# A transformer layer on one core: the first feature block's shift by one-column TensorE products, c spread from a 4 KB row, another order at the start

## The chip, the cores and the metric

The kernel runs on one core of a Trainium2 chip. Its time is the device time of one execution in microseconds (us). Beside it stands the profile of one execution: a hardware record of what each engine did and when. The engines are TensorE (PE; its weight loads are listed as PEld), VectorE (DVE), ScalarE (ACT), GpSimd (POOL) and SyncE (SP), which here only issues DMAs. Each engine works through its own instructions in the order in which they stand in the program, and waits on semaphores for others.

## The reference

One layer of a diffusion transformer over 1024 tokens of 1024 features, with 256 context tokens. Only its beginning matters here:

```python
mod = jax.nn.silu(c) @ w_mod[l] + b_mod[l]
shift1, scale1, gate1, shift2, scale2, gate2 = jnp.split(mod[:, None, :], N_MOD, axis=-1)
...
h = x * (1.0 + scale1) + shift1
...
proj = h @ w_in + b_in
q_b = _rope_2d(_qk_rms(heads(OFF_QB, OFF_KB, B_HEADS), q_norm_g), rope)
```

`c` is one vector of 1024 numbers. A shift and a scale are needed for each of the 1024 features before a feature of `h` exists, and `h` is the operand of every projection. The projection that comes first in the kernel is that to the queries of the global branch (512 columns).

## The kernel before, in words

`x` lies transposed: features on the 128 partitions in KT = 8 blocks of 128 features, tokens along the free axis. Each block `k` of this first stage goes through the same steps.

- **Loads (`load1`, `load_w`, all from SP).** `wm0_k` and `wm1_k` are the columns of `w_mod` that make the shift and the scale of block `k`, 128 x 1024 numbers or 512 KB each; `xr_k` is the block of x, 512 KB; `wr_k` is the block of the projection's weights, 256 KB. So a block needs 1.75 MB. The loads of blocks 0 to 2 are issued at once and those of block `k + 3` while block `k` is worked on. A load waits for one of eight semaphore lanes (that is, for the load eight places ahead of it to have landed), and for its buffer.
- **Products (`product(j, k)`, on DVE, line 193).** Shift (j = 0) and scale (j = 1) of block `k` are sums over 1024 products per partition: `wm` times `sc`, where `sc` holds silu(c) on every partition alike. The result is one column of `modc`, with the bias from `bmc`. Each is one long instruction and a short one that reads its accumulator.
- **Spreading c.** `spread_load` loads the 4 KB row of `c` onto all 128 partitions, half from SP's queue and half from ACT's, 512 KB in all (line 182), and ACT takes the silu (line 185).
- **The affine step (`modulate(k)`).** ACT writes `hh_k` = x * scale + shift rounded to the matmul type (line 241, `high`), and the same unrounded back into `xr_k` (line 242). DVE subtracts the two into `hl_k`, the remainder (line 245, `low`). The weights are split in the same way into a high part (`whqb`) and a low part (`wlqb`). For block 0 the split is on DVE and POOL, for the others on ACT and DVE.
- **Matmuls.** For each block there are 24 of 128 x 512: for eight groups of 128 tokens the products hh x wh, hh x wl and hl x wh, which add up in eight PSUM tiles `q1acc0` to `q1acc7` over the eight blocks: 192 in the stage. They go by halves: four token groups (hh x wh, hh x wl by turns, lines 303 and 304, then four hl x wh, line 306), then the other four.
- **Ahead of them**, PE runs 28 matmuls of ones into `q1acc7` (line 280), whose result is overwritten.

The order on every engine here is the order of the code, written out by hand (a region with a manual schedule), so a diff of code is a diff of the engines' queues. After the stage come the gate products (`g`, lines 90 to 92), whose weights are split on ACT (`whg`) and POOL (`wlg`).

Of the kernel before, what the change touches and what calls it, by code (L numbers as in the profile page):

```python
# [7 lines left out]
F32 = mybir.dt.float32  # L8
R32 = mybir.dt.float32r
AF = mybir.ActivationFunctionType  # L10
ALU = mybir.AluOpType
# [58 lines left out]
def layer_kernel(  # L70
    ctx: ExitStack,
    tc: tile.TileContext,
    xT, ctxT, c_row, cc_row, wmodT, bmod, w_kv, w_qa, w_qb, w_g, b_kv, b_qa, b_qb, b_g,
    sink, qg, kg, w_a, w_b, w_out, ln1, ln2, ln2_row, w_up, conv, convb, w_dn,
    rope_c, rope_s, ident_in, mask_in, out,
):
# [127 lines left out]
    wr1 = {}  # L204

    def load1(k):
        wm = []
        for j in (0, 1):
            w = tmp(f"wm{j}_{k}")
            nc.sync.dma_start(w, wmodT[j * 8 + k])  # L210
            wm.append(w)
        x = tmp(f"xr{k}")
        if k == 0:
            nc.sync.dma_start(x[:, 0:HALF], xT[k][:, 0:HALF])
            load_w(0)
            nc.sync.dma_start(x[:, HALF:T], xT[k][:, HALF:T])
        else:
            nc.sync.dma_start(x, xT[k])
        if k + 1 < KT:
            load_w(k + 1)  # L220
        st1[k] = wm, x

    def product(j, k):
# [2 lines left out]

    def modulate(k):
        last = k + 1 == KT
        if k:
            if not last:  # L230
                w0.append([ph1.tile([P, 512], R32, tag="wp", name=f"w{a}qb{k + 1}", bufs=8) for a in "hl"])
                nc.scalar.copy(w0[-1][0], wr1[k + 1])
            if k > 1:
                product(1, k)
# [5 lines left out]
        def high(s):  # L240
            nc.scalar.activation(hh[:, s], x[:, s], AF.Identity, bias=a, scale=b)
            nc.scalar.activation(x[:, s], x[:, s], AF.Identity, bias=a, scale=b)

        def low(s):
            nc.vector.tensor_tensor(out=hl[:, s], in0=x[:, s], in1=hh[:, s].bitcast(F32), op=ALU.subtract)

        if k == 0:
            product(1, 0)
            w = [ph1.tile([P, 512], R32, tag="wp", name=f"w{a}qb0", bufs=8) for a in "hl"]
            split(wr1[0], *w, nc.vector, nc.gpsimd)  # L250
            w0.append(w)
            high(slice(0, HALF))
            high(slice(HALF, T))
            product(0, 1)
            low(slice(0, HALF))
            product(1, 1)
            low(slice(HALF, T))
            w0.append(wsplit(wr1[1], "qb1"))
        else:
            high(slice(0, T))  # L260
            if not last:
                nc.vector.tensor_tensor(out=w0[-1][1], in0=wr1[k + 1], in1=w0[-1][0].bitcast(F32), op=ALU.subtract)
# [6 lines left out]
    loads.enter_context(tc.manual_schedule(engines={E.SP, E.PE, E.DVE, E.Activation, E.Pool}))  # L269
    nc.scalar.dma_start(bmc, bmod)  # L270
# [4 lines left out]
    nc.vector.tensor_scalar(out=bmc[:, 8:16], in0=bmc[:, 8:16], scalar1=1.0, scalar2=None, op0=ALU.add)  # L275
    for k in (1, 2):
        load1(k)
    acc = [acc_tile(f"q1acc{t}") for t in range(NT)]
    for _ in range(NWARM):
        nc.tensor.matmul(acc[-1][:, 0:P], onesf, onesf, start=True, stop=True)  # L280
    w0 = []
    product(0, 0)
    modulate(0)
    mtmp = pw("mtmp")
    for k in range(KT):
        if k + 3 < KT:
            load1(k + 3)
        if k == 5:
            spread_load(cc_row, 1, (nc.sync,))
            bias_qb = bias_tile(b_qb, "bias_qb")  # L290
        if k + 1 < KT:
            modulate(k + 1)
        else:
            spread(scc, 1)
        h, w = hT[k], w0[k]
        for a in (0, 4):
            ts = [slice(t * P, (t + 1) * P) for t in range(a, a + 4)]
            if k == KT - 1:
                for t, s in enumerate(ts):
                    mm3(acc[a + t], (h[0][:, s], h[1][:, s]), w, False, True)  # L300
                continue
            for t, s in enumerate(ts):
                nc.tensor.matmul(acc[a + t], h[0][:, s], w[0], start=k == 0, stop=False)
                nc.tensor.matmul(acc[a + t], h[0][:, s], w[1], start=False, stop=False)
            for t, s in enumerate(ts):
                nc.tensor.matmul(acc[a + t], h[1][:, s], w[0], start=False, stop=False)

    def constants():
        nc.sync.dma_start(bgc, b_g)
# [1520 lines left out]
def _arrange(i):  # L1830
    import numpy as np

    def A(a):
        return np.ascontiguousarray(a)

    x = np.asarray(i["x"])[0]
    ctx = np.asarray(i["ctx"])[0]
    w_mod = np.asarray(i["w_mod"])[0]
    w_in = np.asarray(i["w_in"])[0]
    b_in = np.asarray(i["b_in"])[0]  # L1840
    w_up = np.asarray(i["w_up"])[0]
# [32 lines left out]
    a = dict(  # L1874
        xT=A(x.T).reshape(KT, P, T),
        ctxT=A(ctx.T).reshape(KT, P, NC),
        c_row=A(np.asarray(i["c"])[0]),
        cc_row=A(np.asarray(i["c_ctx"])),
        wmodT=A(w_mod.T).reshape(48, P, D),
        bmod=A(col(np.asarray(i["b_mod"])[0])),  # L1880
        w_kv=A(w_in[:, kv]).reshape(KT, P, 512),
        w_qa=A(w_in[:, qa]).reshape(KT, P, 512),
        w_qb=A(w_in[:, qb]).reshape(KT, P, 512),
        w_g=A(tiles(w_in[:, 1536:])),
        b_kv=A(b_in[kv]),
        b_qa=A(b_in[qa]),
        b_qb=A(b_in[qb]),
        b_g=A(col(b_in[1536:])),
        sink=A(np.asarray(i["attn_sink"])[0]),
        qg=A(np.asarray(i["q_norm_g"])[0]),  # L1890
        kg=A(np.asarray(i["k_norm_g"])[0]),
        w_a=A(pair(np.asarray(i["w_branch_a"])[0])),
        w_b=A(pair(np.asarray(i["w_branch_b"])[0])),
        w_out=A(tiles(np.asarray(i["w_out"])[0])),
        ln1=A(np.concatenate([col(np.asarray(i["ln1_g"])[0]), col(np.asarray(i["ln1_b"])[0])], 1)),
        ln2=A(np.concatenate([col(np.asarray(i["ln2_g"])[0]), col(np.asarray(i["ln2_b"])[0])], 1)),
        ln2_row=A(np.stack([np.asarray(i["ln2_g"])[0], np.asarray(i["ln2_b"])[0]])).reshape(2, 2, HALF),
        w_up=A(up),
        conv=A(cw.reshape(3, 2 * NF, P).transpose(2, 1, 0)),
        convb=A(col(np.asarray(i["conv_b"])[0])),  # L1900
        w_dn=A(dn),
        rope_c=A(cs.reshape(NT, P, HD).transpose(1, 0, 2)),
        rope_s=A(sn.reshape(NT, P, HD).transpose(1, 0, 2)),
        ident_in=np.eye(P, dtype=np.float32),
        mask_in=A(mask),
    )
    return a
# [29 lines left out]
```

## Time and profile before

| what | value |
|---|---|
| three runs | 1523.26, 1525.3, 1524.3 us; median 1524.3 |
| the profiled execution | 1523.1 us, of which the span of the instructions is 1521.3 us |
| granted TensorE clock in it | 0.997 |
| DVE, ACT, POOL busy | 77%, 52%, 49% of the span |
| HBM read and written | 179.45 MB, 65.86 MB |

The span runs from the first to the last instruction; the profiled execution's own time holds 1.8 us around it. A row of the timeline gives the start, the busy time, the engine, the line and operation, the written tile and the read ones with their shapes, how many rows are merged, and in brackets how long the engine sat idle ahead of it and what released it. `f32 x1` at the end is the type and the count.

### The profile page before, as it was taken

Reading aid. Unit: us, or ns where it says so; the run is one execution under the profiler, and the core shown is the slowest. Engines: PE = TensorE matmul, PEld = TensorE weight load, DVE = VectorE, ACT = ScalarE, POOL = GpSimd, SP = SyncE. Lnnn points to the kernel's source line nnn. Section 1 sums busy time; section 2 is a strip of 40 time slices with the busy share of each in tenths; the row PEclk is TensorE's granted clock in tenths of the full one; section 3 lists DMA queues with packets and bytes.
Section 4 is the critical chain, followed back from the end, with each engine's and each line's share of the span. In section 5 each row is a group of like instructions: output and inputs, shape, how many; then the busy total and the mean of one; then the engine's idle time right before and its main releaser. Section 6 shows DMA issues by size and latency. Waiting matters only on the chain.

```text
span 1521.3 us, 22183 instructions
## 1 busy us (share of the span) xinstructions
PE 1503.2 (99%) x7812; PEld 1263.3 (83%) x7812; DVE 1168.3 (77%) x1751; ACT 786.1 (52%) x1303; POOL 751.3 (49%) x727
## 2 busy tenths in 40 slices
PE   8999999999999999999999999999999999999997
PEld 7888888888988888887888998888888888888887
DVE  6667986539988787877865788888888888557884
ACT  5322222439988677667234555444444444435552
POOL 0356532426776677766124346666666773111121
PEclk9999999999999999999999999999999999999998
DMA  9777672322234576653541322333344448996731
GB/s 370 266 242 242 223 252 87 106 82 68 67 108 104 131 172 167 153 121 89 207 160 42 104 77 98 111 111 111 111 111 111 112 111 238 340 271 210 255 105 56
DMA packets 114399, 232.09 MB, mean 153 GB/s; under 512 B 13200, under 2 KB 28048, under 8 KB 114192
## 3 DMA queue, kind: packets, MB, share of 16 engines
q1 hardware_dynamic: 99056, 201.82, 39.8%
q0 software_dynamic: 10400, 20.19, 8.8%
q10 hardware_dynamic: 4832, 8.68, 1.5%
q8 instruction: 61, 1.00, 0.3%
q14 instruction: 50, 0.41, 0.1%
HBM read 179.45 MB, written 65.86 MB: 161 GB/s over the span
## 4 chain that ended last, share of the span: by engine, by line
PE 92%; DVE 3%; ACT 2%; issue 1%; DMA 1%; POOL 1%; SPq 0%; DVEq 0%; ACTq 0%; POOLq 0%
PE ptr L604 5%; PE p L90 4%; PE p L91 4%; PE p L92 4%; PE g L90 4%; PE g L92 4%; PE g L91 4%; PE av L627 4%; PE av L628 3%; PE b L90 3%; PE b L92 3%; PE b L91 3%; PE s L496 3%; PE s L497 3%; PE c L90 2%; PE c L92 2%
## 5 line engine op out<-in xcount | busy, mean ns | idle before, releaser
L616 DVE TENSOR_TENSOR ptl<-ptr,pth 128x512 fp32r<-128x512 f32 x195 | 128.2, 685 | 20.2 <-ACT pth L615 18.0
L547 ACT ACTIVATE p<-p,nm 128x1280 f32<-128x1280 f32 (+2 forms) x128 | 139.8, 1093 | 6.6 <-DVE p L545 5.9
L87 DVE TENSOR_TENSOR ld<-rd,hd 128x1024 fp32r<-128x1024 f32 x77 | 94.8, 1250 | 50.5 <-ACT hd L82 48.3
L615 ACT CAST pth<-ptr 128x512 fp32r<-128x512 f32 x195 | 111.3, 590 | 30.3 <-PE ptr L604 28.7
L82 ACT CAST hd<-rd 128x1024 fp32r<-128x1024 f32 x77 | 79.3, 1048 | 82.2 <-PE p L92 55.7
L604 PEld LDWEIGHTS ptr<-identr,pb 128*128 128x128 f32 x944 | 96.3, 140 | 23.7 <-ACT pb L550 3.0
L604 PE MATMUL ptr<-identr,pb 128*128 128x128 f32 x944 | 107.5, 245 | 1.5 <-ACT pb L550 1.0
L87 POOL TENSOR_TENSOR wlg<-wg,whg 128x512 fp32r<-128x512 f32 x32 | 48.6, 1529 | 121.7 <-ACT whg L82 80.8
L627 PE MATMUL av<-pth,VT 128*128 128x512 f32 x236 | 104.2, 441 | 0.5 <-ACT side L639 0.3
L90 PE MATMUL p<-hd 128*128 128x512 f32 x264 | 103.2, 391 | 0.0
L92 PE MATMUL p<-hd,ld 128*128 128x512 f32 x264 | 102.8, 389 | 0.0
L91 PE MATMUL p<-ld,hd 128*128 128x512 f32 x264 | 102.7, 389 | 0.0
L90 PE MATMUL g<-hh,whg 128*128 128x512 f32 x256 | 99.9, 390 | 0.0
L92 PE MATMUL g<-hh,wlg 128*128 128x512 f32 x256 | 99.7, 389 | 0.0
L91 PE MATMUL g<-hl,whg 128*128 128x512 f32 x256 | 99.6, 389 | 0.0
L628 PE MATMUL av<-ptl,VT 128*128 128x512 f32 x236 | 97.5, 413 | 0.3 <-DVE ptl L616 0.2
L545 DVE TENSOR_SCALAR_CACHE_REDUCE p<-s,cvt,nmc 128x1024 f32<-128x1024 f32 x64 | 84.2, 1317 | 5.2 <-PE s L497 5.2
L496 PE MATMUL s<-KL,q 128*128 128x512 f32 (+2 forms) x192 | 73.6, 384 | 1.3 <-DVE p L545 0.8
L497 PE MATMUL s<-KL,q 128*128 128x512 f32 (+2 forms) x192 | 71.8, 374 | 0.0
L783 ACT ACTIVATE sg<-g,bgc 128x512 f32<-128x512 f32 x32 | 22.0, 686 | 96.2 <-PE g L92 91.4
L82 ACT CAST wS<-s 128x512 fp32r<-128x512 f32 x76 | 45.3, 620 | 48.7 <-POOL s L1236 47.9
L82 ACT CAST wA<-ru 128x512 fp32r<-128x512 f32 x57 | 35.5, 623 | 62.6 <-PE d L92 33.6
(434 smaller groups left out, 4866.9 us busy)
## 6 DMA issues: line engine op xcount, KB each, us to landing
wml<-in_wmodT_dram SPq DMA_DIRECT2D x48, 512.0 KB
ru<-in_w_up_dram SPq DMA_DIRECT2D x38, 512.0 KB
rd<-td SPq DMA_DIRECT2D x55, 256.0 KB
rd<-sd SPq DMA_DIRECT2D x44, 256.0 KB
rd<-in_w_dn_dram SPq DMA_DIRECT2D x33, 256.0 KB
wm<-in_wmodT_dram SPq DMA_DIRECT2D x16, 512.0 KB
wg<-in_w_g_dram SPq DMA_DIRECT2D x32, 256.0 KB
sgd<-sg ACTq DMA_DIRECT2D x32, 256.0 KB
```

Source lines behind the costliest of these rows:

```text
L82: nc.scalar.copy(hi, src)
L87: lo_eng.tensor_tensor(out=lo, in0=src, in1=hi.bitcast(F32), op=ALU.subtract)
L90: nc.tensor.matmul(ps, a[0], b[0], start=start, stop=False, skip_group_check=resumed)
L91: nc.tensor.matmul(ps, a[0], b[1], start=False, stop=False, skip_group_check=resumed)
L92: nc.tensor.matmul(ps, a[1], b[0], start=False, stop=stop, skip_group_check=resumed)
L496: nc.tensor.matmul(o, self.q[0][:, hs], ks, start=True, stop=False)
L497: nc.tensor.matmul(o, self.q[1][:, hs], ks, start=False, stop=stop)
L547: nc.scalar.activation(row, row, AF.Exp, bias=self.nm[:, hs], scale=-1.0, accum_out=self.sm[:, hs])
L604: i = nc.tensor.transpose(tr[:, h * P:(h + 1) * P], self.bits[:, h, n * P:(n + 1) * P], identr)
L616: nc.vector.tensor_tensor(out=lo, in0=tr, in1=hi.bitcast(F32), op=ALU.subtract)
L627: nc.tensor.matmul(self.av, v, hi, start=first, stop=False)
L628: nc.tensor.matmul(self.av, v, lo, start=False, stop=self.left == 0)
```

## The change

It touches only the first stage. In the order of the program:

- `c` comes twice, each time once from HBM: as one row of 4 KB on partition 0 (ACT's queue, ahead of `bmc`) and as a column tile `ccol`, 128 x 8 (SP's queue, 4 KB). The two loads of 256 KB each are gone.
- 28 matmuls of ones become 7, then 2, then 3. Between the first two lots PE multiplies a row of ones on one partition with the row of `c`, twice 512 columns, which spreads `c` to all partitions in PSUM; ACT takes the silu from there into `sc`, half by half. Between the last two lots stand eight one-column products: block 0's shift, from `wsh0` (the same 1024 x 128 part of `w_mod` as before, laid out with the summed index on the partitions, 512 KB) and from silu of `ccol`. DVE adds the bias. So block 0's shift leaves the DVE products; its scale stays there.
- Order of loads: `wsh0`, `wm1_0`, `wr0`, then x's halves; and `wr1` between `wm0_1` and `wm1_1`.
- The weights of block 0 are split by ACT and DVE, no longer by DVE and POOL.
- `hh` comes in parts for blocks 0 and 1 (256, 256, 512 tokens), and for block 2 (512, 512); the unrounded value comes by halves between them, and `hl` by halves.
- Matmuls: block 0 by halves as before, but in each half first all hh x wh, then all hh x wl, then hl x wh. From block 1 to 6 this order runs over all eight token groups. The number of matmuls of the stage is the same.

```diff
-NWARM = 28
+NWARM = 7, 2, 3
...
+        if k < 3:
+            high(*((q0, q1) if k < 2 else (lo,)))
+            plain(lo)
+            high(hi)
+            plain(hi)
+            if k < 2:
+                w_low(k)
+                w_high()
+                if k:
+                    product(0, 2)
+            if k > 1:
+                w_low(k)
+                w_low(k + 1)
+                product(0, k + 1)
+            low(lo)
+            if k == 0:
+                product(0, 1)
+            low(hi)
...
+    nc.scalar.dma_start(rows[0][0:1], c_row.unsqueeze(0))
+    nc.sync.dma_start(ccol, c_col)
     nc.scalar.dma_start(bmc, bmod)
-    spread_load(c_row, 0, (nc.sync, nc.scalar))
     nc.scalar.activation(negsink[:, 0:1], onec, AF.Silu)
     load1(0)
-    spread(sc, 0)
+    warm(0)
+    nc.scalar.activation(ccol, ccol, AF.Silu)
+    for a in (0, 1):
+        hs = slice(a * HALF, (a + 1) * HALF)
+        nc.tensor.matmul(acc[5 + a], onesf[0:1], rows[0][0:1, hs], start=True, stop=True)
+        nc.scalar.activation(sc[:, hs], acc[5 + a], AF.Silu)
...
+    nc.scalar.copy(w0[0][0], wr1[0])
+    warm(1)
+    for k in range(KT):
+        nc.tensor.matmul(acc[7][:, 0:1], st1[0][0][0][:, k * P:(k + 1) * P], ccol[:, k:k + 1], start=k == 0, stop=k == KT - 1)
+    warm(2)
+    product(1, 0)
+    nc.vector.tensor_tensor(out=modc[:, 0:1], in0=acc[7][:, 0:1], in1=bmc[:, 0:1], op=ALU.add)
     modulate(0)
...
+        for g in (range(0, 4), range(4, 8)) if k == 0 else (range(0, 8),):
+            for m, n in ((0, 0), (0, 1), (1, 0)):
+                for t in g:
+                    nc.tensor.matmul(acc[t], h[m][:, ts[t]], w[n], start=k + m + n == 0, stop=False)
```

On PE, the first instructions of the program before. `onesf` is a tile of ones, and the number behind a name is the block or the token group:

```order
L280 MATMUL q1acc7_187<-onesf_71 128x128 x28
L303 MATMUL q1acc0_180<-whqb0_220,hh0_217 128x512
L304 MATMUL q1acc0_180<-wlqb0_221,hh0_217 128x512
L303 MATMUL q1acc1_181<-whqb0_220,hh0_217 128x512
L304 MATMUL q1acc1_181<-wlqb0_221,hh0_217 128x512
```

The same place of PE now:

```order
L303 MATMUL q1acc4_165<-onesf_71 128x128 x7
L309 MATMUL q1acc5_166<-row0_147,onesf_71 128x512
L309 MATMUL q1acc6_167<-row0_147,onesf_71 128x512
L303 MATMUL q1acc4_165<-onesf_71 128x128 x2
L318 MATMUL q1acc7_168<-ccol_146,wm0_0_152 128x1 x8
L303 MATMUL q1acc4_165<-onesf_71 128x128 x3
L343 MATMUL q1acc0_161<-whqb0_200,hh0_220 128x512
L343 MATMUL q1acc1_162<-whqb0_200,hh0_220 128x512
```

Two products with a row and eight with a column now stand ahead of the first real matmul, and the low weight part is asked for four matmuls later, not at the second.

On DVE, before, from the bias of the scales to the products of block 1 (each product is a long `ISA` row and a short one that reads the sum; `wm0` is a shift's, `wm1` a scale's):

```order
L193 ISA wm0_0_151,modc_60<-wm0_0_151,sc_142,bmc_61 128x1024
L193 ISA wm1_0_153,modc_60<-wm1_0_153,sc_142,bmc_61 128x1024
L86 CAST whqb0_220<-wr0_157 128x512
L193 ISA wm0_1_164,modc_60<-wm0_1_164,sc_142,bmc_61 128x1024
L245 TENSOR_TENSOR hl0_218<-xr0_155,hh0_217 128x512
L193 ISA wm1_1_166,modc_60<-wm1_1_166,sc_142,bmc_61 128x1024
```

The same place of DVE now:

```order
L193 ISA wm1_0_153,modc_60<-wm1_0_153,sc_142,bmc_61 128x1024
L321 TENSOR_TENSOR modc_60<-q1acc7_168,bmc_61 128x1
L238 TENSOR_TENSOR wlqb0_201<-wr0_157,whqb0_200 128x512
L259 TENSOR_TENSOR hl0_221<-xr0_154,hh0_220 128x512
L193 ISA wm0_1_182,modc_60<-wm0_1_182,sc_142,bmc_61 128x1024
L193 ISA wm1_1_183,modc_60<-wm1_1_183,sc_142,bmc_61 128x1024
```

One long product has gone, a 128 x 1 addition has come, and block 0's first remainder now stands ahead of block 1's shift.

On ACT, before, from c to block 1:

```order
L185 ACTIVATE sc_142<-row0_147 128x1024
L241 ACTIVATE hh0_217<-xr0_155,modc_60 128x512
L242 ACTIVATE xr0_155<-xr0_155,modc_60 128x512
L82 CAST whqb1_232<-wr1_160 128x512
L232 CAST whqb2_245<-wr2_170 128x512
L241 ACTIVATE hh1_248<-xr1_168,modc_60 128x1024
L242 ACTIVATE xr1_168<-xr1_168,modc_60 128x1024
```

The same place of ACT now:

```order
L306 ACTIVATE ccol_146<-ccol_146 128x8
L310 ACTIVATE sc_142<-q1acc5_166 128x512
L310 ACTIVATE sc_142<-q1acc6_167 128x512
L315 CAST whqb0_200<-wr0_157 128x512
L253 ACTIVATE hh0_220<-xr0_154,modc_60 128x256 x2
L256 ACTIVATE xr0_154<-xr0_154,modc_60 128x512
L235 CAST whqb1_218<-wr1_186 128x512
L253 ACTIVATE hh1_244<-xr1_184,modc_60 128x256 x2
L256 ACTIVATE xr1_184<-xr1_184,modc_60 128x512
L253 ACTIVATE hh1_244<-xr1_184,modc_60 128x512
```

Block 1's `hh` was one instruction over all tokens; its second half now stands behind the unrounded first half.

More of the change, by code (lines that the diff above doesn't have):

```diff
@@ L206, in load1 @@
     def load1(k):
[L207 to L211, printed above, removed]
+        wm = [tmp(f"wm{j}_{k}") for j in (0, 1)]
         x = tmp(f"xr{k}")
+        nc.sync.dma_start(wm[0], wmodT[k] if k else wsh0)
+        if k == 1:
+            load_w(1)
+        nc.sync.dma_start(wm[1], wmodT[8 + k])
         if k == 0:
+            load_w(0)
             nc.sync.dma_start(x[:, 0:HALF], xT[k][:, 0:HALF])
-            load_w(0)
             nc.sync.dma_start(x[:, HALF:T], xT[k][:, HALF:T])
@@ L218, in load1 @@
             nc.sync.dma_start(x, xT[k])
[L219 to L220 removed]
+            if k + 1 < KT:
+                load_w(k + 1)
         st1[k] = wm, x
@@ L228, in modulate, with w_high, w_low @@
         last = k + 1 == KT
-        if k:
+        lo, hi = slice(0, HALF), slice(HALF, T)
+        q0, q1 = slice(0, 256), slice(256, HALF)
+        if not last:
+            w0.append([ph1.tile([P, 512], R32, tag="wp", name=f"w{a}qb{k + 1}", bufs=8) for a in "hl"])
+        def w_high():
+            nc.scalar.copy(w0[k + 1][0], wr1[k + 1])
+        def w_low(n):
+            nc.vector.tensor_tensor(out=w0[n][1], in0=wr1[n], in1=w0[n][0].bitcast(F32), op=ALU.subtract)
+        if k > 1:
             if not last:
[L231 to L234, printed above, removed]
+                w_high()
+            product(1, k)
+        elif k:
+            product(1, 1)
         hh = hTp.tile([P, T], R32, tag="hT", name=f"hh{k}", bufs=16)
@@ L245, in low @@
             nc.vector.tensor_tensor(out=hl[:, s], in0=x[:, s], in1=hh[:, s].bitcast(F32), op=ALU.subtract)
[L247 to L258, printed above, removed]
+        if k < 3:
[5 more added lines that the diff above has]
+                w_low(k)
+                w_high()
+                if k:
+                    product(0, 2)
+            if k > 1:
+                w_low(k)
[5 more added lines that the diff above has]
+            low(hi)
         else:
             high(slice(0, T))
+            plain(slice(0, T))
             if not last:
-                nc.vector.tensor_tensor(out=w0[-1][1], in0=wr1[k + 1], in1=w0[-1][0].bitcast(F32), op=ALU.subtract)
+                w_low(k + 1)
                 product(0, k + 1)
@@ L269, in layer_kernel, with warm @@
     loads.enter_context(tc.manual_schedule(engines={E.SP, E.PE, E.DVE, E.Activation, E.Pool}))
+    ccol = ph1.tile([P, KT], F32, tag="ccol", name="ccol")
+    rows[0] = ht("row0")
+    hput("row0")
+    nc.scalar.dma_start(rows[0][0:1], c_row.unsqueeze(0))
+    nc.sync.dma_start(ccol, c_col)
     nc.scalar.dma_start(bmc, bmod)
-    spread_load(c_row, 0, (nc.sync, nc.scalar))
     nc.scalar.activation(negsink[:, 0:1], onec, AF.Silu)
     load1(0)
-    spread(sc, 0)
+    acc = [acc_tile(f"q1acc{t}") for t in range(NT)]
+    def warm(n):
+        for _ in range(NWARM[n]):
+            nc.tensor.matmul(acc[4][:, 0:P], onesf, onesf, start=True, stop=True)
+    warm(0)
[4 more added lines that the diff above has]
+        nc.scalar.activation(sc[:, hs], acc[5 + a], AF.Silu)
     nc.vector.tensor_scalar(out=bmc[:, 8:16], in0=bmc[:, 8:16], scalar1=1.0, scalar2=None, op0=ALU.add)
@@ L277, in layer_kernel @@
         load1(k)
[L278 to L282, printed above, removed]
+    w0 = [[ph1.tile([P, 512], R32, tag="wp", name=f"w{a}qb0", bufs=8) for a in "hl"]]
+    nc.scalar.copy(w0[0][0], wr1[0])
[5 more added lines that the diff above has]
+    nc.vector.tensor_tensor(out=modc[:, 0:1], in0=acc[7][:, 0:1], in1=bmc[:, 0:1], op=ALU.add)
     modulate(0)
@@ L295, in layer_kernel @@
         h, w = hT[k], w0[k]
[L296 to L301, printed above, removed]
-            for t, s in enumerate(ts):
[L303 to L306, printed above, removed]
+        ts = [slice(t * P, (t + 1) * P) for t in range(NT)]
+        if k == KT - 1:
+            for t, s in enumerate(ts):
+                mm3(acc[t], (h[0][:, s], h[1][:, s]), w, False, True)
+            continue
+        for g in (range(0, 4), range(4, 8)) if k == 0 else (range(0, 8),):
+            for m, n in ((0, 0), (0, 1), (1, 0)):
+                for t in g:
+                    nc.tensor.matmul(acc[t], h[m][:, ts[t]], w[n], start=k + m + n == 0, stop=False)
     def constants():
```

10 lines of the change are left out of this document (7 added, 3 removed).

## The prediction

> **What bounds the kernel now.** I read the page first, then the list of PE's waits, then the chain of waits over the first 110 us.
>
> ```profile
> span 1521.3 us, 22183 instructions
> PE 1503.2 (99%) x7812; PEld 1263.3 (83%) x7812; DVE 1168.3 (77%) x1751; ACT 786.1 (52%) x1303; POOL 751.3 (49%) x727
> PE 92%; DVE 3%; ACT 2%; issue 1%; DMA 1%; POOL 1%; SPq 0%; DVEq 0%; ACTq 0%; POOLq 0%
> ```
>
> PE is the bound for the whole program, so the change can win only what PE loses in the first stage. The list of PE's waits (us in total, times, longest) shows how little is lost elsewhere:
>
> ```profile
> PE q1acc L303 <- ACT hh L241: 1.6, 1, 1.6
> PE ptr L604 <- ACT pb L550: 1.0, 3, 0.5
> PE q1acc L306 <- DVE hl L245: 0.9, 1, 0.9
> PE q1acc L304 <- POOL wlqb L87: 0.4, 1, 0.4
> ```
>
> The `q1acc` rows are this stage. Nothing else of this size stands in the list, so what PE finishes earlier here should be kept to the end. In the chain the stage hangs on a transfer:
>
> ```profile
> 5.28 6.94 DMA wm<-in_wmodT_dram
> 12.25 1.28 DVE wm L193
> 13.54 0.61 DVE hl L245
> 14.20 1.21 PE q1acc L306 x4
> ```
>
> That is: loads, DVE's product for block 1, the remainder of block 0, PE. The timeline of PE shows the rest:
>
> ```profile
> 10.57 0.51 PE L303 MATMUL q1acc<-whqb,hh 128*128 128x512 f32 x1 [1.62 <-ACT hh L241]
> 23.59 0.39 PE L303 MATMUL q1acc<-whqb,hh 128*128 128x512 f32 x1
> 23.81 0.39 PE L304 MATMUL q1acc<-wlqb,hh 128*128 128x512 f32 x1
> 56.23 0.39 PE L90 MATMUL g<-hh,whg 128*128 128x512 f32 x1
> ```
>
> Block 2 starts at 23.59 and the next stage at 56.23. 144 matmuls lie between, 0.227 us each: PE does not wait there at all. The loss sits between 10.57 and 23.59, where 48 matmuls (10.9 us) take 13.0 us, and ahead of 10.57.
>
> **The change, part by part.** I work out T, the moment when ACT starts block 0's `hh`, and then the path from T to the end of the stage. Before, T was 9.71:
>
> ```profile
> 5.40 1.06 ACT L185 ACTIVATE sc<-row 128x1024 f32<-128x1024 f32 x1 [2.17 <-DMA row<-in_c_row_dram]
> 7.09 1.28 DVE L193 CUSTOM_DVE_ANT_0 wm<-wm,sc,bmc 128x1024 f32<-128x1024 f32 x1 [4.39 <-DMA wm<-in_wmodT_dram]
> 8.38 1.29 DVE L193 CUSTOM_DVE_ANT_0 wm<-wm,sc,bmc 128x1024 f32<-128x1024 f32 x1
> 9.59 0.08 DVE L193 DVE_READ_ACCUMULATOR2_ANT modc<- 128x1 f32 x1
> 9.71 0.81 ACT L241 ACTIVATE hh<-xr,modc 128x512 fp32r<-128x512 f32 x1 [3.25 <-DVE modc L193]
> 10.55 0.81 ACT L242 ACTIVATE xr<-xr,modc 128x512 f32<-128x512 f32 x1
> 11.27 0.80 ACT L241 ACTIVATE hh<-xr,modc 128x512 fp32r<-128x512 f32 x1
> ```
>
> Two products in a row ran from 7.09 to 9.59. Now the scale's runs alone, and I call its start P. It needs `wm1_0` and `sc`.
>
> *wm1_0.* Before, `wm0_0` stood behind 512 KB of rows and landed at 7.05. Now `wm1_0` stands behind the 512 KB of `wsh0`, in the same place: 7.05 at the old pace. The old pace was slow at first, as the rates show (the second last column is the DMA share, the last GB/s):
>
> ```profile
> 3.00:5.00 2.00, 2.00 (x16) 2.00 (x16) 0.00 (x0) 0.22 (x2) 0.00 (x0) 1.00 0.86 221
> 30.00:46.00 16.00, 16.00 (x72) 13.26 (x71) 13.65 (x19) 9.34 (x9) 0.00 (x0) 1.00 1.03 403
> ```
>
> Either that was the row of `c` being read 128 times, then it is gone, and the 0.4 MB missing in those 2 us come 0.9 us sooner (6.1); or it is how the queues start. I keep both ends.
>
> *sc.* 14 passes of ones come first (two rows of the trace for each product). Their price is in two windows, the clock full by its column in both:
>
> ```profile
> 1.08:4.30 3.22, 3.22 (x16) 3.22 (x17) 1.00 0.65 182
> 4.30:9.00 4.70, 4.65 (x42) 4.46 (x40) 1.00 0.99 357
> ```
>
> 16 passes in 3.22 us at first (0.20 each), then some 40 in 4.45 us (0.11): PE is at half speed until about 4.3 whatever the clock column says. So the first lot ends at 1.08 + 2.8 = 3.9. The 4 KB row is there by then, if it lands like the small `bmc`, issued at the same moment:
>
> ```profile
> 2.52 0.17 DVE L275 TENSOR_SCALAR bmc<-bmc 128x8 f32<-128x8 f32 x1 [1.49 <-DMA bmc<-in_bmod_dram]
> ```
>
> The spreading is two products, taken as two passes each, over 512 columns. Not shown in the trace; the bounds are 0.23 us a pass (a 512-column matmul at full speed) and 0.45 (twice that). At 0.27, nearest the full speed that begins in them, it ends at 5.0. ACT's silu of the second half follows at 5.3 and takes about 0.65 (between 0.59 of a 512-column cast from PSUM and 0.81 above): sc is ready at 6.0, 6.7 at worst.
>
> So P lies between 6.0 and 7.1; I take 6.6. From product start to `hh` were 1.33 us (8.38 to 9.71); the 128 x 1 addition between adds 0.17 (the 128 x 8 row above; the bounds are 0.08, the accumulator read, and 0.24). **T = 6.6 + 1.5 = 8.1**, between 7.5 and 8.6.
>
> What must hide under that: the shift's column products wait for `wsh0` (5.4 at the latest, when the first 512 KB had landed before) and for 4 passes of ones (0.11 each, from 5.0 to 5.45), then 16 passes at 0.11, the price of a 128-column pass, end at 7.2, and 0.3 later DVE can add: 7.5, while the scale's product holds DVE until 7.8. Cover: 0.3 us. Bounds of a pass are 0.05 and 0.58, of which more below. Block 0's weights and the first half of x have 1.25 and 1.5 MB ahead of their end; before, 1.5 MB had landed by 8.38, so they allow 8.1 to 8.4. The split's low part, 1.28 us on POOL before (PE waited 0.4 for it), is one DVE instruction of 0.69 behind the addition, done at T + 0.6; PE asks for it at T + 1.6. Hidden.
>
> From T on:
>
> ```profile
> L1230 ACT ACTIVATE v<-z,lnx 128x256 f32<-128x256 f32 x16 | 9.4, 587 | 0.0
> 12.25 1.28 DVE L193 CUSTOM_DVE_ANT_0 wm<-wm,sc,bmc 128x1024 f32<-128x1024 f32 x1 [2.21 <-DMA wm<-in_wmodT_dram]
> 13.46 0.69 DVE L245 TENSOR_TENSOR hl<-xr,hh 128x512 fp32r<-128x512 f32 x1
> 14.06 1.28 DVE L193 CUSTOM_DVE_ANT_0 wm<-wm,sc,bmc 128x1024 f32<-128x1024 f32 x1
> ```
>
> - ACT: two quarters of `hh0` (0.59 each, 0.5 from start to start), the unrounded half from T + 1.1 to T + 1.95. PE starts at T + 0.65 (10.57 - 9.71, less 0.2 for the shorter piece) and has eight matmuls until T + 2.5, then waits 0.2 for the remainder.
> - DVE by starts (1.21 a product, 0.60 a remainder, as above): remainder T + 1.98, shift of block 1 T + 2.58, remainder T + 3.79, scale of block 1 T + 4.39, so ACT's `hh1` at T + 5.72. PE ends block 0 at T + 6.35 and gets its first piece at T + 6.37: no wait, where 14.20 stood at the end of a 0.9 us one.
> - **A new wait.** PE now goes over all eight token groups with hh x wh first, so it wants the second half of `hh1` after four matmuls, at T + 7.3. ACT has that half behind two quarters and the unrounded first half (by starts 0.5, 0.62, 0.72): T + 7.57, and 0.86 later (9.71 to 10.57) PE can go: T + 8.43. It stands 1.15 us.
> - Behind it 20 matmuls of block 1 and 144 of the others at 0.227: 37.2. The stage ends at **T + 45.6 = 53.7**. Blocks 2 on: `hh2` at T + 11.2, its second half for PE at T + 13.6, wanted at T + 13.9; after that each block costs DVE 4.6 us and PE 5.44, so PE is not caught up.
>
> The loads permit it: product 12.25 waited for its DMA, and without 512 KB at 403 GB/s it may start 1.3 sooner, 10.95, against T + 2.58 = 10.7. Block 1's scale and x land 1.3 and 2.6 later, 12.25 and 13.55, against T + 4.39 = 12.5 and T + 5.72 = 13.8. So at this pace a T below 7.9 would not help.
>
> The next stage's first weights are ready:
>
> ```profile
> 49.52 1.65 ACT L82 CAST whg<-wg 128x512 fp32r<-128x512 f32 x3
> 50.20 2.54 POOL L87 TENSOR_TENSOR wlg<-wg,whg 128x512 fp32r<-128x512 f32 x2 [38.80 <-DMA gcol<-in_qg_dram]
> ```
>
> First halves at 50.1 and 51.5, and not later than that now. The fewer ones matmuls and loads cost nothing by themselves.
>
> **Sum:** 56.23 - 53.7 = 2.5 us gained. Profiled execution 1523.1 - 2.5 = 1520.6; the median of the runs lies 1.2 above that execution, so **1521.8**. By T's ends the gain is 2.0 to 3.1.
>
> **The rivals.**
>
> *The transfers are not earlier.* If the slow start belongs to the queues and `wsh0` with its 128 small pieces of `ccol` ahead fares no better, `wm1_0` lands when it did, by 8.25 (its product at 8.38 did not wait). T = 9.75, gain 0.9: 1523.4. For it: 221 GB/s at 0.86 share. Against: half a MB less stands ahead of it.
>
> *PE still slow at the head.* The 0.20 us passes ended at 4.3 after 16 passes without a gap. If PE stays slow through the new head, spreading takes 4 x 0.45 (5.7), the ones 0.8 (6.5), 16 column passes 3.2 (9.7), T = 10.2: gain 0.4, 1523.9. Half-speed matmuls of block 0 are then largely taken up by the 1.15 us wait.
> The Trainium skill, TensorE: Matmul & The Clock Gate, Part 1, says that the gate opens after about 3.4 us of sustained work, by a window that runs free of the kernel. The 3.2 us above agree. By the phase of that window the step could come later than here, which is this rival.
>
> *Column products in single file: slower.* With one column there is no long matmul to cover the load of the next 128 x 128 weights. A pass of ones lasted 0.58 at most:
>
> ```profile
> L280 PE MATMUL q1acc<-onesf x56: 274/275/580, 1.1 to 8.7; 128*128 128x128 f32 x56
> ```
>
> If the 16 passes stood in single file at that, they would end at 5.45 + 9.3 = 14.75, T = 15.2, the stage at 60.8: 4.6 slower, 1528.9. It decides from 0.29 a pass (no gain) and 0.48 (0.2% lost). Against: 40 such passes took 0.11 each, one behind the other.
>
> *More than 2.5.* Full pace of the loads from the start (P = 6.0, T = 7.5) and shorter ACT pieces at the new wait, of which each 0.1 us is 0.1 us of the end: 3.1 to 4, 1520.7 as its middle.
>
> **How the numbers follow.** 0.2% of the time, 3.05 us, is about what a measurement of this kernel can tell from no change. My forecast has 0.52, transfers no earlier 0.12, PE slow at the head 0.08: all within 0.2%, together 0.72. More than 3.05 gained: 0.23, since T's lower end just reaches it. Slower by the column products: 0.05. The range goes from 1520.2 (gain of 3.1 and the spread of the runs, 1 us) to 1524.1, which takes in the two weak cases.
>
> **What would show it.** In the changed profile: the product of line 193 for the scale starts at 6.0 to 7.1; `hh0` at 7.5 to 8.6; column products end by 7.5; PE waits about 1.1 us once in block 1 for the second `hh` half, on ACT, and not for loads; `g` starts at 53.2 to 54.2. Wrong would be: a wait of `modc`'s addition on PE, a PE wait from block 2 on, or a later stage that waits where none did.

## The result, and the profile after

The changed kernel takes **1534.06 us** (median of six runs, 1532.15 to 1536.02), the kernel before, beside it, 1524.53 us (six runs, 1523.26 to 1525.5). The ratio is 1.0065, with an interval from 1.0054 to 1.0076: slower by 9.5 us, where 2.5 us of gain were forecast. The profiled execution after took 1536.02 us, the slowest of the six.

The page of the changed kernel begins with its span and the busy time of each engine:

```profile
span 1533.9 us, 22170 instructions
PE 1518.3 (99%) x7800; PEld 1267.7 (83%) x7800; DVE 1167.7 (76%) x1752; ACT 789.1 (51%) x1312; POOL 753.3 (49%) x726
PE 93%; DVE 3%; ACT 2%; issue 1%; POOL 1%; DMA 0%; DVEq 0%; ACTq 0%; POOLq 0%; SPq 0%
```

PE has 12 instructions fewer than before and is busy for 15.1 us longer (1503.2 before), while the span grew by 12.6. So PE did not lose the time by waiting. The list of its waits says the same:

```profile
PE q1acc L303 <- DVE mhalf L118: 1.1, 1, 1.1
PE ptr L641 <- ACT pb L587: 0.9, 2, 0.5
PE s L533 <- DVE p L582: 0.8, 3, 0.3
PE av L665 <- POOL ptl L87: 0.7, 1, 0.7
```

Before, three waits in `q1acc` made up 2.9 us; they are all gone. That looks like a success, and is none. The timeline of the changed kernel shows what stands in their place at the head:

```profile
1.08 3.36 PE L303 MATMUL q1acc<-onesf 128*128 128x128 f32 x14 [1.08 <-DVE mhalf L118]
4.37 3.78 PE L309 MATMUL q1acc<-row,onesf 1*128 1x512 f32 x4
6.48 0.60 ACT L310 ACTIVATE sc<-q1acc 128x512 f32<-128x512 f32 x1 [3.19 <-PE q1acc L309]
8.07 1.22 PE L303 MATMUL q1acc<-onesf 128*128 128x128 f32 x4
8.18 0.60 ACT L310 ACTIVATE sc<-q1acc 128x512 f32<-128x512 f32 x1 [1.11 <-PE q1acc L309]
8.81 1.28 DVE L193 CUSTOM_DVE_ANT_0 wm<-wm,sc,bmc 128x1024 f32<-128x1024 f32 x1 [3.51 <-ACT sc L310]
9.09 3.41 PE L318 MATMUL q1acc<-ccol,wm 128*128 128x1 f32 x16
12.54 0.16 DVE L321 TENSOR_TENSOR modc<-q1acc,bmc 128x1 f32<-128x1 f32 x1 [2.44 <-PE q1acc L318]
12.73 0.60 ACT L253 ACTIVATE hh<-xr,modc 128x256 fp32r<-128x256 f32 x1 [3.45 <-DVE modc L321]
13.64 2.05 PE L343 MATMUL q1acc<-whqb,hh 128*128 128x512 f32 x4
59.76 0.40 PE L90 MATMUL g<-hh,whg 128*128 128x512 f32 x1
```

The four passes that spread `c` hold PE for 3.78 us and the 16 column passes for 3.41 us. So `hh0` starts at 12.73 and not at 9.71, and the first real matmul at 13.64 and not at 10.57. The next stage (`g`) starts at 59.76, 3.53 us later than before. Of the 12.6 us of the span, 9 are still to be found behind that.

They show in no wait and in no idle time, only in the time of one matmul. The list of groups has, before:

```profile
L90 PE MATMUL g<-hh,whg 128*128 128x512 f32 x256 | 99.9, 390 | 0.0
L91 PE MATMUL g<-hl,whg 128*128 128x512 f32 x256 | 99.6, 389 | 0.0
L90 PE MATMUL p<-hd 128*128 128x512 f32 x264 | 103.2, 391 | 0.0
```

and after:

```profile
L90 PE MATMUL g<-hh,whg 128*128 128x512 f32 x256 | 101.5, 397 | 0.0
L91 PE MATMUL g<-hl,whg 128*128 128x512 f32 x256 | 101.2, 395 | 0.0
L90 PE MATMUL p<-hd 128*128 128x512 f32 x264 | 103.2, 391 | 0.0
```

The numbers behind the bar are busy us and the mean of one in ns. The groups of `g`, which read `hh` or `hl`, have gone up by 6 or 7 ns, and the group `p`, of the same shape in a later stage, has not moved. From start to start, ten products in a row, first of the kernel before:

```profile
99.75 0.39 PE L90 MATMUL accqa<-whqa,hh 128*128 128x512 f32 x1
...
102.01 0.39 PE L91 MATMUL accqa<-wlqa,hh 128*128 128x512 f32 x1
```

then of the changed one:

```profile
99.65 0.39 PE L90 MATMUL accqa<-whqa,hh 128*128 128x512 f32 x1
...
101.98 0.39 PE L91 MATMUL accqa<-wlqa,hh 128*128 128x512 f32 x1
```

That is 2.26 us for ten against 2.33. Over windows of 12 us the means are **0.2267 and 0.2333 us**, in every window between the head and the last of these products that holds no others. 192 of them make the queries of the first stage and 1152 the stages up to some 340 us; 1344 x 0.0066 = 8.9 us. The last product that reads `hh` shows the sum, before and after:

```profile
332.24 0.39 PE L92 MATMUL g<-hh,wlg 128*128 128x512 f32 x1
```

```profile
343.16 0.40 PE L92 MATMUL g<-hh,wlg 128*128 128x512 f32 x1
```

It is 10.9 us later. The rest of the span, 1190.7 us for 1189.1, holds 1.7 us more: in this execution the granted clock fell to half for 3.4 us, a window that the profile prints as

```profile
350.90:354.30 3.40, 3.40 (x17) 0.50 0.21 74
```

(the third column from the end is the granted clock). Such a single fall is in some of the executions below, of kernels of either pace (`a_best`, `b_col` and `b_newmm` at 0.2267, `a_ones14` and `b_pad32` at 0.2333), and not in others, so it is left out of what follows.

### The profile page after: what moved, and what is told of

Same layout as the page of the kernel before. It is cut to its first block, busy times and chain, and to the rows that moved or that the text cites. A ratio compares the mean times of both kernels' runs of the same rounds, so it can differ in the third digit from the quotient of the medians.

```text
span 1533.9 us, 22170 instructions
## 1 busy us (share of the span) xinstructions
PE 1518.3 (99%) x7800; PEld 1267.7 (83%) x7800; DVE 1167.7 (76%) x1752; ACT 789.1 (51%) x1312; POOL 753.3 (49%) x726
## 4 chain that ended last, share of the span: by engine, by line
PE 93%; DVE 3%; ACT 2%; issue 1%; POOL 1%; DMA 0%; DVEq 0%; ACTq 0%; POOLq 0%; SPq 0%
PE ptr L641 5%; PE p L90 4%; PE g L90 4%; PE p L92 4%; PE p L91 4%; PE g L92 4%; PE g L91 4%; PE av L664 4%; PE av L665 3%; PE b L90 3%; PE b L91 3%; PE b L92 3%; PE s L533 3%; PE s L534 3%; PE q1acc L343 3%; PE c L90 2%
```

## The experiments

Nothing in the change touches a matmul of a later stage. The theories were: one of the new one-partition products (ROW) or one-column products (COLUMN) leaves PE in a slower manner; the clock's rise, now at 16.4 us inside the real work, does (GATE); the new order of the products does (ORDER); the waits that PE used to have in the stage, and now has not, set the pace (PAUSE); or the layout of the memory does (ADDRESS). A time below without an interval or a number of runs is that of one execution; there the pace in the trace decides, over more than a thousand products.

### The new products and the clock

Into the kernel before, behind its ones, went two one-partition products (`b_row`), or eight one-column products (`b_col`):

```diff
+    for n in (0, 1):
+        nc.tensor.matmul(acc[5 + n], onesf[0:1], rows[0][0:1, n * HALF:(n + 1) * HALF], start=True, stop=True)
```

```diff
+    for _ in range(KT):
+        nc.tensor.matmul(acc[7][:, 0:1], onesf, onesf[:, 0:1], start=True, stop=True)
```

> The kernel before with two products added behind its 28 products of ones: a row of ones on one partition times the row of c on one partition, 512 columns each, into PSUM that is overwritten later. Theory ROW (a product over one partition leaves TensorE in a slower pace for 512-column matmuls until its clock next drops): blocks 2 to 7 go at 0.233 us a matmul, as in the changed kernel, not 0.227; the first real matmul comes at most 1 us later; in all 7 to 11 us slower than before. Theory GATE (the pace depends on whether the clock rises during the stream of 512-column matmuls): the clock rises at about 4 us, among the ones, so the pace stays 0.227 and the time is within 2 us of before.

> The kernel before with eight products of one column (ones times a column of ones) behind its 28 products of ones. Theory COLUMN (a one-column product leaves TensorE in the slower pace): 0.233 us a matmul and 7 to 11 us slower. Theories ROW and GATE: 0.227 us and the time within 2 us of before.

The times were 1524.81 and 1525.82 us beside 1524.83, and the pace stayed at 0.2267 in both. ROW and COLUMN fall. The two runs also give the prices that the prediction had to bound, with PE at full speed. In `b_row` and in `b_col`:

```profile
10.46 1.98 PE L282 MATMUL q1acc<-row,onesf 1*128 1x512 f32 x4
```

```profile
9.08 1.84 PE L282 MATMUL q1acc<-onesf 128*128 128x1 f32 x16
```

A one-partition pass takes 0.48 us from start to start (10.46 to the first real matmul at 12.37, by four), a one-column pass 0.11.

For GATE, the kernel before got 3 ones in place of 28, so that the clock rises late, and the changed kernel 14 ones in place of its first 7, so that it rises early (`NWARM`).

> The kernel before with 3 products of ones instead of 28, nothing else. Theory GATE: the clock rises only among the real matmuls (about 3.4 us behind their start, near 14 us), and the pace behind that is 0.233 us until the clock next drops: 7 to 12 us slower. Theories ROW and COLUMN: the pace is 0.227 us behind the rise; only the first matmuls are at half speed, 1 to 2 us slower than before.

> The changed kernel with 14, 2 and 3 products of ones instead of 7, 2 and 3. All theories: the clock rises at about 4 us, inside the first lot, so the spreading takes half as long (0.43 us a pass, 1.7 us in all) and a column pass 0.11 us or less; block 0's hh starts near 9.5 instead of 12.7. Theory GATE: the pace is then 0.227 us, the time within 2 us of before. Theories ROW and COLUMN: the pace stays 0.233 us, 5 to 9 us slower than before.

`b_ones3` took 1523.14 us. The clock rose at 14.3 us, inside block 0, and the real matmuls ahead of that went at half speed, about 0.43 us each. Yet the pace afterwards was 0.2267 and `g` started at 56.24, as before. A slow start of PE costs nothing where PE would wait anyway: its waits for `wlqb` and `hl` (0.4 and 0.9 us before) shrank to 0.1 and to nothing. `a_ones14` took 1536.08 us at 0.2333, although its clock rose at 6.0. GATE falls. But the clock did not stay up, as the windows of `a_ones14` show:

```profile
6.00:9.00 3.00, 3.00 (x14) 1.00 0.99 374
9.30:16.10 6.80, 6.80 (x29) 0.51 1.04 411
16.10:20.00 3.90, 3.90 (x18) 0.98 1.04 408
```

In the first window PE does the one-partition passes and ones, at full clock; just behind it the clock is at half for 6.8 us, under the column passes and the first real matmuls, and PE is issuing all the time. So `hh0` started at 12.62 us, not near 9.5 as expected.

### The order, the wait, the row

`b_newmm` is the kernel before with the changed order of products, `a_oldmm` the changed kernel with the old order (the loops of the diff, exchanged). `a_pause` gives the changed kernel a wait again, by computing `hh4` four times:

```diff
+            if k == 4:
+                for _ in range(3):
+                    high(slice(0, T))
             high(slice(0, T))
```

`a_dmarow` is the changed kernel with `c` spread by DMA as before, without the one-partition products.

> The kernel before with only the changed kernel's order of the matmuls of blocks 0 to 6 (in each lot first all hh x wh, then all hh x wl, then hl x wh, from block 1 over eight token groups). Theory ORDER (an unbroken stream in the new order falls into a rhythm of 0.233 us a matmul and hands it on to the stages behind): 0.233 us from block 1 or 2 on and 7 to 10 us slower than before. Theory HEAD (the rhythm comes from how the stream of the changed kernel starts, and the order has no part in it): 0.227 us, time within 2 us of before.

> The changed kernel with the matmul order of before, all else as changed. Theory ORDER: 0.227 us from block 2 on, the gate products start near 58.4 and the time is 1 to 3 us above before, what the late start of the first matmul (13.6 for 10.6) leaves. Theory HEAD: 0.233 us and 8 to 12 us above before, as the changed kernel.

> The changed kernel with block 4's hh computed four times over, so that TensorE has to wait about 1.8 us for it once, near 37.4; the result is the same. Theory PAUSE (the slow rhythm lives only as long as the stream is unbroken, and the stretch behind a wait may settle at 0.227 in either order): 0.227 us from block 5 on, near 5 us faster than the changed kernel. Theory ORDER in its strict form (the new order always goes at 0.233): 0.233 us behind the wait too, through the stage's end and beyond, 1 to 2 us slower than the changed kernel.

> The changed kernel with c spread as before by two loads of 256 KB; the one-partition products are gone, the one-column products stay. If the head's loss is the one-partition products' length alone, hh of block 0 starts at 9.5 to 10; if it is the clock, which stays low through products that load TensorE little, the column passes still take 0.2 us each, end near 10.5, and hh starts near 10.8. The pace behind: theory ORDER 0.233 us, theory HEAD 0.227 if the one-partition products were part of it.

The times were 1524.73, 1532.33, 1533.93 and 1532.66 us beside 1524.03. The pace was 0.2267 in `b_newmm` and 0.2333 in the other three. In `a_pause` PE did wait:

```profile
36.15 2.13 PE L346 MATMUL q1acc<-whqb,hh 128*128 128x512 f32 x8 [0.87 <-ACT hh L253]
```

and went on at 0.2333 right behind it. ORDER and PAUSE fall, and so does the row once more. Taken one at a time, nothing that the change adds, moves or takes away on PE was left to explain the pace.

The traces show one more thing, about the head. `a_oldmm` and `a_pause` have the changed kernel's instructions on PE up to the first real matmul, and yet their `hh0` started at 9.57 and 9.59 us, not at 12.73. In `a_oldmm`:

```profile
4.36 2.17 PE L309 MATMUL q1acc<-row,onesf 1*128 1x512 f32 x4
7.01 2.33 PE L318 MATMUL q1acc<-ccol,wm 128*128 128x1 f32 x16
9.57 1.09 ACT L253 ACTIVATE hh<-xr,modc 128x256 fp32r<-128x256 f32 x2 [1.87 <-DVE modc L321]
```

Their clock rose at 4.8 and 5.0 us and fell again at 8.2 and 8.4; in the changed kernel's profiled execution it rose at 16.4 only. So that late start is not the program's alone: it hangs on when the clock rises. There is one trace for each kernel, so how often either case comes is not known. (`a_dmarow`, without the one-partition passes, started `hh0` at 9.94.)

### The layout

The diff has one more line: `ccol = ph1.tile([P, KT], F32, ...)`, 32 bytes in each partition. In the built program this tile lies at byte 162592 and has pushed the pool of `hh` and `hl` down: `hh0` stands at byte 96576 of the partition before and at 96544 after, while the weights `whqb0` stand at 168768 in both. `b_pad32` puts such a tile into the kernel before and does nothing with it but clear it once:

```diff
+    pad = ph1.tile([P, KT], F32, tag="pad", name="pad")
+    nc.gpsimd.memset(pad, 0.0)
```

`a_pad64` gives the changed kernel 64 bytes for `ccol`, if only the start on a multiple of 64 counts. `a_full` does this too and spreads `c` by products over all 128 partitions of a cleared tile. `b_align` puts 32 bytes into the pool of constants, which moves the operands of the *later* stages (the pool that holds `row0`, `KL` and others) from a remainder of 32 to a multiple of 64 and leaves `hh`, `hl` and their weights alone:

```diff
+    pad = ctile([P, 8], F32, "pad")
+    nc.gpsimd.memset(pad, 0.0)
```

> The kernel before with one more tile of 32 bytes a partition in the pool of this stage's weights; it is cleared once and never read. Theory ADDRESS: the column tile of the changed kernel (32 bytes) moves all hh and hl tiles from a multiple of 64 bytes to one of 32, while the weights stay on a multiple of 64, and a stream of matmuls whose two operands differ by 32 bytes in this way goes at 0.233 us, not 0.227. So this kernel goes at 0.233 from the first block to about 345 us and is 8 to 10 us slower than before, though no other instruction changes. Any theory that lays the pace on the new instructions, their order or the clock: 0.227, time within 1.5 us of before.

> The changed kernel with the column tile made 64 bytes a partition (half of it unused), so that hh and hl lie on multiples of 64 bytes again. Theory ADDRESS: 0.227 us from block 1 on; 7 to 9 us faster than the changed kernel; against before between 1 us faster and 3 us slower, by when the clock rises in the head. Theory HEAD: 0.233 us and no gain over the changed kernel.

> As the changed kernel with the 64-byte column tile, and c's row spread by a product over all 128 partitions (the tile is cleared first, so 127 of them add zero) in place of one partition. Theory ACTIVITY (the clock rises by how much of the array works; a product over one partition does not count): the clock rises by 8 us at the latest and hh of block 0 starts before 10.5 in every profile; 1 to 3 us faster than the 64-byte kernel without it. If one-partition products count as any other, the two kernels agree within 1 us.

> The kernel before with a tile of 32 bytes more in the pool of constants, which moves the pool behind it (KL, VT, B and others) from 32 to 64-byte multiples; hh and this stage's weights stay. Theory ADDRESS in the form that only the difference of the two operands counts: the later stages, where both operands lie on odd multiples of 32 bytes and go at 0.227 today, get pairs that differ, so their pace falls to 0.233: 4 to 12 us slower than before. In the form that any operand off a 64-byte multiple costs: the later stages get no slower, 0 to 8 us faster.

`b_pad32` took 1533.46 us beside 1524.46, with the old instructions, the old head and the old waits:

```profile
L90 PE MATMUL g<-hh,whg 128*128 128x512 f32 x256 | 101.5, 397 | 0.0
L90 PE MATMUL p<-hd 128*128 128x512 f32 x264 | 103.2, 391 | 0.0
L305 PE MATMUL q1acc<-whqb,hh 128*128 128x512 f32 x56 | 22.3, 398 | 1.5 <-ACT hh L241 1.5
```

32 unused bytes cost 9.0 us in this execution. In its trace the last product that reads `hh` stands at 340.61, 8.4 us later than before, though `hh0` started at 9.62; behind that this execution had a single fall of the clock, from 348.7 to 352.1 us. ADDRESS holds. The guess that a multiple of 64 is what counts does not. `a_pad64` took 1533.26 us (ratio 1.006, 1.0047 to 1.0074): the queries of its first stage and two later groups (`accqb`, `acckb`) went at 0.229, the others that read `hh` or `hl` at 0.2333. And `b_align` was slower than anything, 1536.98 us. Its groups:

```profile
L90 PE MATMUL p<-hd 128*128 128x512 f32 x264 | 104.5, 396 | 0.0
L90 PE MATMUL g<-hh,whg 128*128 128x512 f32 x256 | 99.9, 390 | 0.0
L90 PE MATMUL a<-B,wA 128*128 128x512 f32 x152 | 60.2, 396 | 0.0
```

It is the mirror image of `b_pad32`: now `g` has its 390 ns and `p` and `a` have up to 396. What was moved onto "better" addresses is slow where the tile that it is multiplied with has stayed. Where both have moved it is fast, in the same lines of the same trace. From 730 to 743 us both operands of `b<-O,hwb` start on a multiple of 256 bytes; from 744 to 766 us they are 32 bytes off each other:

```profile
L90 PE MATMUL b<-O,hwb 128*128 128x512 f32 x16 | 6.2, 389 | 0.0
```

```profile
L90 PE MATMUL b<-O,hwb 128*128 128x512 f32 x31 | 12.2, 395 | 0.0
```

So the position of the two operands against each other counts. `a_full` (1532.74 us, ratio 1.0063, 1.0049 to 1.0077) kept the clock up from 9.5 us on, with column passes of 1.84 us, but waited 2.0 us for its row behind the clearing; `hh0` started at 12.28, not before 10.5 as expected, and nothing was gained by it. Its queries, and all its later groups that read `hh` or `hl` except `g`, went at 0.229.

### The changed kernel at the old addresses, and which shift counts

`a_gcol` is the changed kernel word for word, but `ccol` has no tile of its own:

```diff
-    ccol = ph1.tile([P, KT], F32, tag="ccol", name="ccol")
+    ccol = gcol[:, 0, 0:KT]
```

`gcol` stands in both kernels and is loaded much later, so `hh0` is back at 96576. `a_gcol_dmarow` adds to it the spreading by DMA. `b_pad128` and `b_pad512` are `b_pad32` with tiles of 128 and 512 bytes.

> The changed kernel word for word, but the column of c lies in the first 32 bytes of gcol, a tile that both kernels have and that is loaded much later, so that the tiles hh and hl come back to the addresses that they have in the kernel before. ADDRESS (the 32-byte tile is the whole loss of pace): the 512-column products go at 0.2267 us from the first full-speed one on; the head stays as it is (first real matmul near 13.6, half speed until 16.4), the first blocks save 192 x 0.0066 = 1.3 us, so the g products start near 58.5 (56.23 before) and the time is near 1524.5 + 2.3 = 1526.8 us. CODE (something else in the changed program sets the pace too): 0.2333 us, g near 59.8, 1533 to 1536 us. If the late start is caught up later, 1524.5.

> As a_gcol, and c is spread by DMA over all partitions as in the kernel before, without the one-partition products (the column products, the order of loads and of parts stay as changed). With the old addresses: pace 0.2267; first real matmul near 10.6 as it was with the new addresses, g near 56.7 - 1.3 = 55.4, against 56.23 before, so the time is near 1524.5 - 0.8 = 1523.7 us, a gain of 0.05%, within what can be told from no change. CODE: 0.2333, g 56.7, near 1532.7 us.

> The kernel before with an unused tile of 128 bytes, which moves hh and hl down by 128 bytes against the weights. Only the remainder by 32, 64 or 128 counts: pace 0.2267 in all stages, g at 56.2, 1524.5 us. The remainder by 256 or 512 counts (the weight slices lie 512 bytes apart): 0.2333 or something between in the stages that read hh, g between 56.3 and 57.2, 1525 to 1533.5 us.

> The kernel before with an unused tile of 512 bytes, which moves hh and hl down by one whole step of the weight slices. Every theory of relative addresses with a step of up to 512 bytes: pace 0.2267, g at 56.2, 1524.5 us. If a moved base or the extra tile itself costs, whatever its size: 0.2333, g near 57.2, 1533.5 us.

`a_gcol` took **1526.68 us** (eleven runs) beside 1524.65 (ratio 1.0011, 1.0003 to 1.002). Its rows:

```profile
L90 PE MATMUL g<-hh,whg 128*128 128x512 f32 x256 | 99.9, 390 | 0.0
```

```profile
4.37 3.78 PE L309 MATMUL q1acc<-row,onesf 1*128 1x512 f32 x4
9.09 3.41 PE L318 MATMUL q1acc<-gcol,wm 128*128 128x1 f32 x16
12.73 0.60 ACT L253 ACTIVATE hh<-xr,modc 128x256 fp32r<-128x256 f32 x1 [3.45 <-DVE modc L321]
58.53 0.39 PE L90 MATMUL g<-hh,whg 128*128 128x512 f32 x1
334.55 0.39 PE L92 MATMUL g<-hh,wlg 128*128 128x512 f32 x1
```

The head is that of the changed kernel to the hundredth, and the old pace is back. This splits the loss. In the traces the last product that reads `hh` stands at 332.24 before, 334.55 here and 343.16 after: 2.3 us for the head and 8.6 for the addresses. By the medians it is 2.0 us and the other 7.5 of the 9.5. `a_gcol_dmarow` (1524.77 us in eleven runs, ratio 1.0003, 0.9994 to 1.0012) shows by its median that most of the head's loss goes with the one-partition products; `g` started at 56.84, not at the 55.4 expected, since its clock was at half from 7.9 to 14.8.

Of the shifts, 128 bytes cost (1531.61 us, 0.2333 throughout) and 512 did not (1524.93 us, 0.2267). The last two kernels went to the shift between them, and to the question whether the changed parts are worth anything once both losses are out. `a_best` is `a_gcol_dmarow` with the row of `c` and `bmc` loaded first, the column of `c` behind them, and 18, 0 and 3 ones:

> The kernel before with an unused tile of 256 bytes: hh and hl move down by 256 bytes against the weights, half a step of the weight slices. 128 bytes cost as much as 32, 512 nothing. The remainder by 256 counts: pace 0.2267, g at 56.2, 1524.7 us. The remainder by 512 counts: pace 0.2333 (or the 0.229 seen for part of the products at 64 bytes), g near 57.2, 1530 to 1533.5 us.

> The changed kernel with hh and hl at the old addresses (the column of c in gcol), c spread by DMA and the loads' first four in the order of before (the column of c behind them), 18 ones ahead of the column products and none between. HEAD (the changed parts and order are worth something once neither the addresses nor the one-partition products cost): wm0 lands near 7.1, the 16 column passes take 1.84 us at full speed and end near 9.0, the scale product ends near 9.75, first real matmul near 10.5, g near 55.5 (56.23 before), time near 1524.6 - 0.7 = 1523.9 us, ratio 0.9995, which is within what can be told from no change. If the clock falls ahead of the column products they take 3.4 us and end near 10.5, first real matmul near 11.3, g near 56.5, 1524.9 us.

256 bytes cost nothing: 1524.71 us, 0.2267. So here the remainder by 256 of the distance between the two operands decides: shifts of 32, 64 and 128 bytes cost, 256 and 512 do not. In the kernel before, `hh`, `hl` and all their weights have the remainder 64, and the pairs of `p`, `a` and the other large projections of the later stages have 224 on both sides; after, `hh` and `hl` have 32 against 64.

`a_best` took 1523.86 us (eleven runs) beside 1524.33 (ratio 0.9995, 0.9986 to 1.0004): no difference that can be told. In its trace:

```profile
7.62 1.95 PE L313 MATMUL q1acc<-gcol,wm 128*128 128x1 f32 x16 [0.45 <-ACT gcol L304]
9.95 1.09 ACT L253 ACTIVATE hh<-xr,modc 128x256 fp32r<-128x256 f32 x2 [0.47 <-DVE modc L316]
18.36 1.20 PE L338 MATMUL q1acc<-whqb,hh 128*128 128x512 f32 x4 [0.82 <-ACT hh L253]
55.67 0.39 PE L90 MATMUL g<-hh,whg 128*128 128x512 f32 x1
```

`g` stands 0.56 us earlier than before, with `hh0` 0.24 later. In the traces of kernels with the first stage of before and its pace, `g` stands between 55.91 (`b_align`) and 56.29 (`b_pad512`), so part of that is spread. What little there is to gain comes behind the start of `hh0`, so rather from the order of the parts than from the columns; no run takes the two apart.

## Why the prediction was wrong

- **"What PE finishes earlier here should be kept to the end", and 144 matmuls at 0.227 us.** This is the step that failed and cost most. The sum took the pace of the kernel before for the stage and let everything behind it stand. The new 32-byte tile moved `hh` and `hl`, and each of the 1344 products that read them got 6.6 ns longer. The tile had no term in the sum and none among the rivals, and no rival spoke of a later stage. `b_pad32` shows the effect alone, `a_gcol` takes it out: 7.5 of the 9.5 us. Without it the forecast still fails, by the head: `a_gcol` took 1526.68 us, and the range ended at 1524.1.
- **Spreading c, two passes a product, 0.23 to 0.45 us each, 0.27 taken.** The size was off. The upper bound came from matmuls of the rounded type, and this product is of plain f32. A pass took 0.48 us at full speed (`b_row`) and about 0.93 in the changed kernel, at half. So the spreading ended at 8.15 and not at 5.0, and P, the scale's product, came at 8.81 (6.0 to 7.1 foreseen).
- **Column products, 16 passes at 0.11.** Right at full speed: 1.84 us in `b_col`. At half speed they took 3.41. They started at 9.09 and not at 5.45, and did not hide behind the scale's product, with a cover of 0.3 us: DVE waited 2.44 us for them (0.88 in `a_oldmm`). The rival that had them in single file, at 0.58 each, did not come about.
- **The rival "PE still slow at the head"** came about in this execution; the forecast gave it 0.08. It put T, the start of `hh0`, at 10.2; T was 12.73. It had priced the slow spreading at 4 x 0.45 = 1.8 us and it took 3.78; most of the rest is that the row's product began at 4.37 and not at 3.9. The Trainium skill, "TensorE: Matmul & The Clock Gate", Part 1, says that the clock's step hangs on a window of about 3.4 us of sustained work that runs free of the kernel. This case agrees as to the window: in kernels that begin with the same 28 ones the clock rises anywhere from 3.9 (`b_pad32`) to 7.3 us (`b_row`), and where it changes more than once in the head it stays up or down for 3.4 or 6.8 us at a time. So the rise at 4.0, on which the sum built its price of a pass, was one case of several. This case does not bear out that busy time alone opens the gate, since in the changed kernel PE was busy without a gap from 1.08 on, and the clock rose at 16.4.
- **From T on, T + 45.6.** Right as a sum, in part by luck. In `a_gcol` it was 58.53 - 12.73 = 45.8, in `a_best` 55.67 - 9.95 = 45.7. The new wait for the second half of `hh1`, forecast at 1.15 us, is there in `a_best` with 0.82. In the changed kernel and in `a_gcol` it did not appear: half-speed matmuls, up to 16.4 and 16.3, had used the time, as that rival said. So in `a_gcol` the sum agrees with one of its terms replaced by another.
- **The transfers.** DVE's scale product waited for `sc` and not for its load, so whether `wm1_0` came earlier never mattered.

Of the miss of 12.3 us, some 7.5 are a mechanism that the sum did not have. Most of the rest is T, which in the profiled execution came 4.6 us late, at 12.73 and not at 8.1, by passes priced too low and a clock that stayed at half. In `a_oldmm`, where the clock was up from 4.8 to 8.2, the same head had T at 9.57, still later than 8.6, the end of T's range.

## What to carry to other kernels

A new tile is an edit of its own, however small: look where it pushes its neighbours, and compare the pace of one unchanged matmul group before and after, in a stage that the change does not touch. Before such a kernel is judged, its new tiles can be laid into existing ones, which here turned a loss of 9.5 us into 2.0. And a short product at the start of a program has two prices, that of the full and that of the half clock, and the second is to be planned with: here the same head paid now one, now the other.

## What the hardware showed

- **Relative addresses set the pace of PE.** In the long streams here, 0.2267 us for a 128x512 product where the distance between its two operands is a multiple of 256 bytes, 0.2333 (2.9% more) where it is off by 32 or 128, with no wait, no idle time and the same mean weight load (188 ns) in the profile. The Trainium skill, "TensorE: Matmul & The Clock Gate", Part 2, says that loading the next weights takes no read bandwidth from the running matmul, since each has a port of its own. Here the one does not go untouched by the other, or something else in that path depends on the address; which, no run shows. At 64 bytes the distance does not settle it: `accqa` and `accka` had 0.2333 in `a_pad64` and 0.229 in `a_full`, at the same addresses; why is open too. Nor does it settle it in short stretches: stretches of 12 products of equal remainder between slow ones, in `b_align`, went at 0.228 to 0.231. In both kernels `VT` and `pth`, the operands of line 627 before, lie 128 bytes off each other by that remainder; whether their 236 products would gain from being moved wasn't tried.
- **The clock can fall under a PE that never pauses.** In `a_ones14` it fell to half at 9.4 us, behind one-partition passes, and stayed there through the column passes; in `a_oldmm` and `a_pause` it fell so at 8.2 and 8.4. The column passes alone did not bring it down in `a_best`, where it rose at 4.9 and stayed up through the head. With products over all 128 partitions (`a_full`) it rose at 9.5 and stayed up, with the same number of passes. These kernels differ in more than that, so it is a hint and not shown that the one-partition passes do it.
- **Before the first change of the clock the profile's column says 1.00**, even where PE goes at half speed: in the changed kernel the window from 9 to 12.3 us has 1.00, and the 16 column passes that start at 9.09 take 3.41 us. The pace of equal passes is the better witness at the start of a trace.
